# A decoder layer's down projection by Strassen's seven products, with GpSimd making the operand sums

## The chip, the cores and the metric

One core of one Trainium2 chip runs the whole layer. The metric is device time in microseconds (us) from launch to end, the median of several runs. A core has TensorE (PE, with its weight loads PEld), VectorE (DVE), ScalarE (ACT), GpSimd (POOL) and SyncE (SP, which here only issues DMAs). Each engine works through its own queue in order and waits for others by semaphores. TensorE writes to PSUM, which has eight banks of 128 x 512 f32. The profile shows one execution.

## The reference

One layer: attention and a short convolution feed a first residual, then comes the feed-forward part, which is what the change touches. S = 2048 tokens, D = 1024, DFF = 2816, all f32.

```
x  = x + g1 * (mixed @ w_out)
h2 = rmsnorm(x, norm2_g) * (1 + sc2) + sh2
u  = causal_dwconv(h2 @ w_up, ffn_conv_w)      # w_up: 1024 x 5632, three taps over tokens
u_gate, u_val = split(u, 2)
y  = (silu(u_gate) * u_val) @ w_down           # w_down: 2816 x 1024
x  = x + g2 * y                                # g2: one gate per column
```

## The kernel before

The kernel works by token halves `hv` of 1024 tokens. For each there is an up stage and a down stage, and the four stand in a row at the end: up 0, down 0, up 1, down 1. Before them lie the projections, attention and the output projection, which do not change; a norm of token blocks 0 and 1 (`norm2`) runs beside the latter.

**Up stage** (`up`). DFF is cut into NPAIR = 22 tiles of 128 channels. A tile `i` computes the gate and the value channels for 1024 tokens, itself by Strassen's seven products in f16 high and low parts: seven products of 12 matmuls of 512 columns, 84 in all, into three PSUM accumulators X, Y and Z, of `ps_d` and `ps_u` in turn. Beside tile i, `up_weights(i + 1)` forms the next tile's weights: two 128x1024 loads of w_up on SP's queue, scaled by ScalarE, four sums on VectorE, and high and low parts (ScalarE casts, VectorE subtracts: `high`, `low`). VectorE and ScalarE also read the accumulators, run the convolution (`tap`, `taps`), the silu, and the product of gate and value, in `finish`, which is stepped while the next tile's products run. VectorE has 18 instructions in a tile. Four have an accumulator in PSUM as one operand; the other 14 have both tensors in SBUF. The result, 128 channels x 1024 tokens, is stored to `y_sc[i]` in DRAM. GpSimd has nothing to do in the four stages.

**Down stage** (`down`). Per half there are four parts `n` (two blocks of 512 tokens times two halves of 512 columns), each over 22 tiles: 88 steps. A step loads 128 x 512 of y and 128 x 512 of w_down into one 128x1024 tile (`load_pair`), splits it into a high and a low part in fp32r (`split_pair`: ScalarE, then VectorE), three steps ahead, and runs 12 matmuls: four token tiles of 128, three products each (high by high, high by low, low by high). Four accumulators of `ps_d` gather 22 tiles. `add_gated` then multiplies by the gate and adds x, two VectorE instructions per accumulator, and stores the output. `side` is stepped at every other step: in the first down stage it holds the end of the up stage, `norm2` of token blocks 2 and 3 (in `columns` each of 16 groups is four transposes into the one bank of `ps_n`, which ScalarE then reads), and the first weights of up stage 1.

`K` keeps an instruction at its place in program order; what has none may be moved by the scheduler, as the w_up loads are, which SP issues about a tile ahead.

## Time and profile before

| what | us |
|---|---|
| median of 3 runs (lowest, highest) | 2444.38 (2442.55, 2447.06) |
| span of the profiled execution | 2437.6 |
| first up stage, from about 1144 | 399 |
| first down stage, from about 1543 | 252 |
| second up stage, from about 1795 | 398 |
| second down stage, from about 2193 to the end | 245 |

The profiled execution's span lies 6.8 us below the median of the runs: the time of a run has the start and the end of the program in it, outside the first and last instruction. The clock that TensorE was granted was 0.997 of full speed over the span. An engine's busy time in a stretch says how much of it the engine worked; a group row gives the instructions of one line with their number, sum and mean, and behind the bar the idle time ahead of them with what ended it. Durations of matmuls overlap, so the pace of TensorE is read from the chain, which counts each stretch once.

### The profile page before, as it was taken

What the parts mean: (1) busy time and instruction counts of PE and PEld (TensorE: products, weight loads), DVE (VectorE), ACT (ScalarE), POOL (GpSimd) and SP (SyncE); (2) the same over time, 40 slices, a digit from 0 to 9 for tenths busy, and PEclk for the clock granted to TensorE, in tenths of its full rate; (3) what the DMA queues carried; (4) which work ended last, traced back from release to release, by engine and by line L of the source; (5) the groups of instructions that cost most, each with busy time, mean ns of one, the idle gap of its engine ahead of it and who ended that gap; (6) DMA issues with size and microseconds to landing.
All of it is one profiled execution on the core that took longest, in us unless ns stands there. A gap on an engine that the chain in (4) does not pass through costs nothing.

```text
span 2437.6 us, 38399 instructions
## 1 busy us (share of the span) xinstructions
PE 2360.2 (97%) x14451; PEld 1586.8 (65%) x14451; DVE 1772.6 (73%) x3329; ACT 1261.4 (52%) x2024; POOL 336.6 (14%) x282
## 2 busy tenths in 40 slices
PE   5999999999899998999999999999999999999999
PEld 5988788888677776444444444788864444448887
DVE  6566884542799987456888888757768888885554
ACT  4433443221588887343665665554546556554333
POOL 0111011011577884001000000000000000000000
PEclk9999999999999999999999999999999999999999
DMA  9344686543599997434222222676742222236775
GB/s 278 118 122 126 181 235 189 155 139 95 116 185 184 225 181 153 166 113 147 84 89 87 87 87 87 204 245 216 229 134 87 87 87 88 93 103 209 229 227 183
DMA packets 428706, 368.70 MB, mean 151 GB/s; under 512 B 184208, under 2 KB 327912, under 8 KB 427496
## 3 DMA queue, kind: packets, MB, share of 16 engines
q1 hardware_dynamic: 421400, 349.40, 51.4%
q10 hardware_dynamic: 4752, 8.46, 1.0%
q0 software_dynamic: 2368, 8.39, 0.9%
q8 instruction: 113, 1.85, 0.3%
q14 instruction: 73, 0.60, 0.1%
HBM read 267.54 MB, written 65.08 MB: 136 GB/s over the span
## 4 chain that ended last, share of the span: by engine, by line
PE 82%; DVE 7%; issue 5%; ACT 3%; DMA 2%; POOL 1%; SPq 0%; ACTq 0%; DVEq 0%; POOLq 0%
PE acc L1256 33%; PE acc L142 27%; PE pr L142 11%; PE pv L142 3%; PE pt L937 2%; PE ps L876 1%; PE ps L877 1%; DVE near L944 1%; PE po L973 1%; DVE s_t L900 1%; ACT s_t L917 1%; PE po L975 1%; PE po L974 1%; PE pt L1097 1%; ACT near L939 0%
## 5 line engine op out<-in xcount | busy, mean ns | idle before, releaser
L1256 PEld LDWEIGHTS <-pair 128*128 128x128 f16 x3696 | 361.6, 98 | 436.1 <-issue 0.3
L1256 PE MATMUL acc<-t,pair 128*128 128x512 f16 x2112 | 477.4, 379 | 0.0
L1256 PE MATMUL acc<-b,pair 128*128 128x512 f16 x1584 | 363.4, 379 | 0.0
L1228 DVE TENSOR_TENSOR lo<-raw,hi 128x1024 fp32r<-128x1024 f32 x176 | 211.8, 1222 | 153.6 <-ACT hi L1227 151.5
L142 PE MATMUL acc<-hi 128*128 128x512 f32 x704 | 276.7, 393 | 1.6 <-DVE t L1073 1.6
L142 PE MATMUL acc<-lo,hi 128*128 128x512 f32 x704 | 274.2, 390 | 0.5 <-DVE lo L1228 0.5
L1227 ACT ACTIVATE hi<-raw 128x1024 fp32r<-128x1024 f32 x176 | 182.4, 1055 | 178.1 <-PE acc L142 142.3
L142 PE MATMUL acc<-hi,lo 128*128 128x512 f32 x704 | 274.2, 389 | 0.0
L1269 DVE SCALAR_TENSOR_TENSOR w<-w,fcw,w 128x1024 f32<-128x1024 f32 x176 | 226.1, 1284 | 34.7 <-ACT w L1264 25.4
L1080 ACT ACTIVATE pair<-raw 128x1024 f16<-128x1024 f32 x132 | 138.3, 1049 | 68.3 <-DVE raw L1163 68.3
L142 PE MATMUL acc<-wp,mp 128*128 128x512 f16 x768 | 171.1, 382 | 1.1 <-DVE raw L829 1.0
L1264 ACT ACTIVATE w<-w,fcw 128x1024 f32<-128x1024 f32 x88 | 100.7, 1144 | 130.7 <-DVE w L1162 130.7
L917 ACT ACTIVATE s_t<-s_t,nb,cst 128x2048 f32<-128x2048 f32 (+15 forms) x128 | 164.7, 1288 | 4.8
L1083 DVE TENSOR_TENSOR pair<-raw,pair 128x1024 f16<-128x1024 f32 x132 | 160.7, 1217 | 4.7 <-ACT pair L1080 4.7
L608 ACT ACTIVATE wx<-wx 128x512 f32<-128x512 f32 x88 | 55.6, 632 | 203.7 <-DMA wx<-in_w_up_dram 173.9
L142 PE MATMUL pr<-hh,wh 128*128 128x512 f32 x384 | 153.3, 399 | 0.0
L142 PEld LDWEIGHTS acc<-hi 128*128 128x128 f32 x704 | 132.2, 188 | 31.5 <-DVE t L1073 4.4
L142 PE MATMUL pr<-hh,wl 128*128 128x512 f32 x384 | 150.8, 393 | 0.6 <-DVE wl L179 0.6
L142 PE MATMUL pr<-hl,wh 128*128 128x512 f32 x384 | 151.0, 393 | 0.0
L142 PEld LDWEIGHTS acc<-hi,lo 128*128 128x128 f32 x704 | 132.2, 188 | 27.7
L142 PEld LDWEIGHTS acc<-lo,hi 128*128 128x128 f32 x704 | 132.2, 188 | 27.6 <-DVE lo L1228 1.1
L929 POOL TENSOR_TENSOR wide<-s_t,wide 128x1024 f16<-128x1024 f32 x64 | 136.7, 2136 | 5.3
(296 smaller groups left out, 4680.9 us busy)
## 6 DMA issues: line engine op xcount, KB each, us to landing
raw<-in_w_up_dram SPq DMA_DIRECT2D x88, 512.0 KB, 3.9
raw<-y_sc SPq DMA_DIRECT2D x176, 256.0 KB, 4.2
raw<-in_w_down_dram SPq DMA_DIRECT2D x176, 256.0 KB, 5.5
wx<-in_w_up_dram SPq DMA_DIRECT2D x88, 256.0 KB, 2.9
y_sc<-w SPq DMA_DIRECT2D x44, 512.0 KB, 2.6
wm<-in_w_ada_dram SPq DMA_DIRECT2D x128, 128.0 KB, 2.9
wr<-in_w_in_dram SPq DMA_DIRECT2D x40, 256.0 KB, 4.2
x_t<-in_x_dram SPq DMA_DIRECT2D x16, 512.0 KB, 5.7
```

What stands on the lines that cost most here:

```text
L142: ins = T.matmul(acc, lhsT=a, rhs=b, start=st, stop=sp)
L608: K(A.activation(t, t, AF.Abs, accum_out=l1[:, n : n + 1]))
L917: K(A.activation(cols, cols, AF.Exp, bias=nb[:, p : p + 1], scale=qk[:, 4:5], accum_out=un["l"][:, p : p + 1]))
L929: K(G.tensor_tensor(wide[:, 1, :], s_t[:, WB * P : WU], wide[:, 0, :], op=ALU.subtract))
L937: K(T.transpose(pt[:, b * P : (b + 1) * P], s_t[:, (b0 + b) * P : (b0 + b + 1) * P], ident))
L1080: K(A.activation(hi, raw, AF.Copy))
L1083: K(V.tensor_tensor(lo, raw, hi, op=ALU.subtract))
L1227: K(A.activation(hi, raw, AF.Copy))
L1228: K(V.tensor_tensor(lo, raw, hi.bitcast(F32), op=ALU.subtract))
L1256: K(T.matmul(acc, lhsT=a, rhs=b, start=st, stop=sp, skip_group_check=True))
L1264: K(A.activation(y, u[:, 0:1024], AF.Copy, scale=fcw[:, ct : ct + 1]))
L1269: K(V.scalar_tensor_tensor(y, u[:, m : m + 1024], fcw[:, m * 44 + ct : m * 44 + ct + 1], y, op0=ALU.mult, op1=ALU.add))
```

## The change

The down stage computes the same product by seven products in place of eight. For a pair j of channel tiles (2j and 2j + 1, NJ = 11 pairs), of y with a and b for its two blocks of 512 tokens and of the gated w_down with its two column halves, it needs seven y operands and seven w operands: b11, b21, b22 and the sums t1 to t4 on the one side, a11, a12, a22 and the sums s1 to s4 on the other.

- In the up stage `finish` writes the product of gate and value into a tile of its own. `down_inputs` stores three parts of it as they are and has GpSimd make t1 at an even tile and t2, t3 and t4 behind an odd one (128x512 f32, four per pair).
- In the first up stage alone, `down_weights` loads two rows of w_down for each pair, has GpSimd multiply them by the gate (two 128x1024 products) and form four 128x512 sums, and keeps them in DRAM for both halves. It is issued at the start of an odd tile.
- The stores of GpSimd's results are issued by SP at the start of the next tile (`store_later`, `flush`).
- `down` has 7 products of 11 steps: 77 steps with one split and 12 matmuls each, as before. Two sets of accumulators alternate, `ps_d` and `ps_u` with the bank of `ps_n`; a set is added to over two or three products, and after each product its four accumulators are read once (`evict`), by ScalarE after the first and by VectorE after the others; GpSimd adds SBUF tiles in twelve places. The output needs no gate any more.
- `side` is stepped at every step, and twice at some; steps that need a bank for transposes run only in the products 1, 3, 4 and 7 (`window`), and the first weights of up stage 1 fill the steps between (`other`).

```diff
-    y_sc = [dram.tile([P, S], F32, name=f"y_sc{i}") for i in range(NPAIR)]
+    y_op = {n: [dram.tile([P, D], F32, name=f"y_{n}_{j}") for j in range(NJ)] for n in ("b11", "b21", "b22", "t1", "t2", "t3", "t4")}
+    w_op = {n: [dram.tile([P, D], F32, name=f"w_{n}_{j}") for j in range(NJ)] for n in ("a11s3", "a12a22", "s1s2", "s4")}
...
-            g = temp()
-            K(V.tensor_tensor(g, acc, gate, op=ALU.mult))
-            K(V.tensor_tensor(src, src, g, op=ALU.add))
-            nc.sync.dma_start(dst, src)
...
+        plan = (("a11", "b11"), ("s2", "t2"), ("a12", "b21"), ("s3", "t3"), ("s1", "t1"), ("a22", "t4"), ("s4", "b22"))
...
+        def load_pair(hv, p, j):
+
+            w, y = plan[p]
+            n, e = place[w]
             raw = raw_tile()
-            K(nc.sync.dma_start(raw[:, 0:512], y_sc[i][:, Q * 512 : (Q + 1) * 512]))
-            K(nc.sync.dma_start(raw[:, 512:1024], w_down[i * P : (i + 1) * P, hf * 512 : (hf + 1) * 512]))
+            K(nc.sync.dma_start(raw[:, 0:512], y_op[y][j][:, hv * 512 : (hv + 1) * 512]))
+            K(nc.sync.dma_start(raw[:, 512:1024], w_op[n][j][:, e * 512 : (e + 1) * 512]))
...
+        def down_inputs(i, hv, y):
+
+            j = i // 2
+            cols = slice(hv * 512, (hv + 1) * 512)
+            a, b = y[:, 0:512], y[:, 512:1024]
+            if i % 2 == 0:
+                t12 = fq.tile([P, 1024], F32, tag="lo", name="t12", bufs=4)
+                K(nc.sync.dma_start(y_op["b11"][j][:, cols], a))
+                gsub(t12[:, 0:512], b, a)
+                store_later(y_op["t1"][j][:, cols], t12[:, 0:512])
...
+            gsub(t12[:, 512:1024], b, t12[:, 0:512])
+            gsub(t34[:, 0:512], b, b12)
+            gsub(t34[:, 512:1024], a, t12[:, 512:1024])
...
+        def down_weights(j):
...
+            for w in (wa, wb):
+                K(G.tensor_tensor(w, w, gates[:, D : 2 * D], op=ALU.mult))
+            gadd(s1, a21, a22)
+            gsub(a21, a11, a21)
+            gsub(s2, s1, a11)
+            gsub(s4, a12, s2)
+            for n, w in (("a11s3", wa), ("a12a22", wb), ("s1s2", wc)):
+                store_later(w_op[n][j], w)
+            store_later(w_op["s4"][j][:, 0:512], s4)
...
-                K(V.tensor_tensor(yv, yg, yv, op=ALU.mult))
-                nc.sync.dma_start(y_sc[i][:, hv * 1024 : (hv + 1) * 1024], yv)
+                y = fq.tile([P, 1024], F32, tag="hi", name="y", bufs=4)
+                K(V.tensor_tensor(y, yg, yv, op=ALU.mult))
+                down_inputs(i, hv, y)
...
+                flush()
+                if hv == 0 and i % 2:
+                    next(wsum)
...
-            todo = [(n, i) for n in range(4 * hv, 4 * hv + 4) for i in range(NPAIR)]
+            todo = [(hv, p, j) for p in range(7) for j in range(NJ)]
...
+                if p == 0:
+                    K(A.activation(u2[t], a, AF.Copy))
+                elif p == 1:
+                    add(u2[t], u2[t], a)
+                elif p == 2:
+                    add(xs[0, 0][t], xs[0, 0][t], a)
+                    write(0, 0, t, xs[0, 0][t])
+                elif p == 3:
+                    add(u3[t], u2[t], a)
+                    gadd(u3[t], u3[t], xs[1, 1][t])
...
+                if j == 0:
+                    if p in (0, 4):
+                        sets["a"] = [ps_d.tile([P, 512], F32, tag="d", name="acc") for _ in range(4)]
+                    elif p in (1, 3):
+                        sets["b"] = [ps_u.tile([P, 512], F32, tag="u", name="acc") for _ in range(3)] + [bank["n"]()]
+                    acc = sets["b" if p in (1, 3, 5) else "a"]
...
-                if e < 3 or e % 2 == 0:
-                    next(side, None)
...
+                window = p in (0, 2, 3, 6) and (p == 0 or j >= 2)
+                spare["bank"] = bank["d" if p == 3 else "n"]
+                for _ in range(2 if p == 2 and j >= 4 else 1):
+                    if need != "bank" or window:
+                        need = next(side, "end")
+                        if need == "end":
+                            next(other, None)
+                    else:
+                        next(other, None)
```

GpSimd's queue at the fourth pair of up 0 (`wd` is w_down, `y` the product of gate and value). Before, its last rows ahead of the program's end are stores of the first residual, and none belongs to the four stages:

```order
L831 DMA x1_sc14_93<-x_q_14753 128x512
L831 DMA x1_sc15_94<-x_q_14754 128x512
L1405 UNCONDITIONAL_BRANCH
L1405 ISA
```

With the change, the same queue has for each pair:

```order
L1298 TENSOR_TENSOR wd_15913<-wd_15913,gates_239 128x1024
L1298 TENSOR_TENSOR wd_15914<-wd_15914,gates_239 128x1024
L1258 TENSOR_TENSOR wd_16026<-wd_15913,wd_15914 128x512
L1261 TENSOR_TENSOR wd_15913<-wd_15913 128x512
L1261 TENSOR_TENSOR wd_16026<-wd_16026,wd_15913 128x512
L1261 TENSOR_TENSOR wd_16027<-wd_15914,wd_16026 128x512
L1261 TENSOR_TENSOR t12_16099<-y_16097 128x512
L1261 TENSOR_TENSOR t12_16099<-y_16252,t12_16099 128x512
L1261 TENSOR_TENSOR t34_16254<-y_16252,y_16097 128x512
L1261 TENSOR_TENSOR t34_16254<-y_16252,t12_16099 128x512
```

Ten instructions per pair are new there; the seventh runs late in the odd tile, the last three in the even tile behind it. In up 1 only these four remain.

TensorE's queue in down 0, at a place where `columns` puts its transposes (`pt`) between the matmuls of two steps. Before, one group of four stands between two steps:

```order
L142 MATMUL acc_17989<-hi_18297,lo_18298 128x512
L1097 MATMUL pt_18364<-ident_117,w4_18090 128x128
L1097 MATMUL pt_18364<-ident_117,w4_18091 128x128
L1097 MATMUL pt_18364<-ident_117,w4_18092 128x128
L1097 MATMUL pt_18364<-ident_117,w4_18093 128x128
L142 MATMUL acc_17986<-hi_18326 128x512
```

With the change, at a place in the third product:

```order
L1479 MATMUL acc_18406<-hi_18980,lo_18981 128x512
L1093 MATMUL pt_19065<-ident_216,w4_18494 128x128
L1093 MATMUL pt_19065<-ident_216,w4_18495 128x128
L1093 MATMUL pt_19065<-ident_216,w4_18496 128x128
L1093 MATMUL pt_19065<-ident_216,w4_18497 128x128
L1093 MATMUL pt_19075<-ident_216,w4_18494 128x128
L1093 MATMUL pt_19075<-ident_216,w4_18495 128x128
L1093 MATMUL pt_19075<-ident_216,w4_18496 128x128
L1093 MATMUL pt_19075<-ident_216,w4_18497 128x128
L1479 MATMUL acc_18403<-hi_19017 128x512
```

Two groups follow each other without a matmul between them; this is so at four places (one in the first product, three in the third).

SP's queue in up 0, at the start of an even tile. Before, the two w_up loads of a tile follow one store:

```order
L1176 DMA raw_16000<-in_w_up_dram 128x8x128
L1282 DMA y_sc6_101<-w4_15873 128x1024
L1176 DMA raw_16142<-in_w_up_dram 128x8x128
L1176 DMA raw_16143<-in_w_up_dram 128x8x128
L1282 DMA y_sc7_102<-w4_16016 128x1024
```

With the change, five stores that wait for GpSimd and two loads stand ahead of them:

```order
L1272 DMA y_b11_5_100<-y_16727 128x512
L1251 DMA w_a11s3_5_177<-wd_16543 128x1024
L1251 DMA w_a12a22_5_188<-wd_16544 128x1024
L1251 DMA w_s1s2_5_199<-wd_16656 128x1024
L1251 DMA w_s4_5_210<-wd_16657 128x512
L1251 DMA y_t1_5_133<-t12_16729 128x512
L1292 DMA wd_16858<-in_w_down_dram 128x1024
L1292 DMA wd_16859<-in_w_down_dram 128x1024
L1172 DMA raw_16999<-in_w_up_dram 128x8x128
```

At the start of an odd tile it is three stores.

123 lines of the change are left out of this document (92 added, 31 removed).

## Prediction

> **What bounds the kernel now.** I read the page's busy row first, then the windows of the four stages that the change touches, then the chain of work in order of time. The columns of the windows are the stretch, its length, and each engine's busy time with its number of instructions.
>
> ```profile
> PE 2360.2 (97%) x14451; PEld 1586.8 (65%) x14451; DVE 1772.6 (73%) x3329; ACT 1261.4 (52%) x2024; POOL 336.6 (14%) x282
> ...
> core 0: us, PE busy (x) PEld busy (x) DVE busy (x) ACT busy (x) POOL busy (x), PEclk, DMA share, GB/s
> 1144.00:1543.00 399.00, 399.00 (x1851) 180.97 (x1849) 347.29 (x388) 233.28 (x346) 1.08 (x2) 1.00 0.28 90
> 1543.00:1795.00 252.00, 249.90 (x1124) 203.99 (x1124) 174.14 (x215) 131.04 (x156) 0.00 (x0) 1.00 0.71 229
> 1795.00:2193.00 398.00, 398.00 (x1846) 180.44 (x1845) 347.31 (x389) 227.68 (x302) 0.00 (x0) 1.00 0.27 88
> 2193.00:2438.00 245.00, 239.90 (x1059) 198.23 (x1057) 130.65 (x123) 91.53 (x87) 0.00 (x0) 1.00 0.67 212
> ...
> 1144.35 398.86 PE acc L1256 x1848
> 1794.64 398.88 PE acc L1256 x1848
> 2193.52 235.32 PE acc L142 x1038
> ```
>
> The stages are, in turn, first up, first down, second up, second down. TensorE has work without a break in all four; in the up stages the chain is one piece of matmuls. A matmul of an up stage takes 398.86 / 1848 = 0.2158 us of the chain, one of a down stage 235.32 / 1038 = 0.2267. But VectorE is close behind in the up stages: 347.3 of 399 us. Per pair of up tiles (11 pairs) it is busy 347.3 / 11 = 31.6 us while TensorE needs 398.86 / 11 = 36.3: a slack of 4.7. GpSimd does nothing there. Its work of the change is put into that slack.
>
> **What the down stages lose.** Each goes from 88 steps of 12 matmuls to 77, so 132 matmuls fewer: 132 x 0.2267 = 29.9 us, twice. The form and the pace stay (same types, same weight loads), and each step still has one split, so VectorE and ScalarE have less to do in step with TensorE. In the second stage nothing but splits lies beside the matmuls:
>
> ```profile
> L1228 DVE TENSOR_TENSOR lo<-raw,hi 128x1024 fp32r<-128x1024 f32 x85 | 103.5, 1224 | 105.5 <-ACT hi L1227 103.7 <-DMA raw<-y_sc 1.5
> ...
> 2432.51 0.39 PE L142 MATMUL acc<-hi,lo 128*128 128x512 f32 x1
> 2432.94 0.69 DVE L1073 TENSOR_TENSOR t<-acc,gates 128x512 f32<-128x512 f32 x1
> 2433.66 0.69 DVE L1074 TENSOR_TENSOR xs<-xs,t 128x512 f32<-128x512 f32 x1
> ```
>
> VectorE idles 105 us between its splits, so the twelve GpSimd additions of that stage find room. At the end one of two VectorE instructions behind the last matmul goes: 0.7. Second down: **-30.6**.
>
> The first down stage also carries the norm of token blocks 2 and 3, with 64 transposes. Before, a step of it came at every other matmul step; now it comes at every step, in product 3 partly two at once, and those with transposes in products 1, 3 and 4 alone.
>
> ```profile
> L1099 ACT ACTIVATE t<-pt,sh,a 128x512 f32<-128x512 f32 x16 | 12.4, 776 | 39.3 <-PE pt L1097 39.3
> ...
> L1083 DVE TENSOR_TENSOR t<-t,t 128x512 f16<-128x512 f32 x16 | 10.6, 686 | 0.0
> ```
>
> At four places eight transposes now stand in a row on one bank, so the second four wait for the first's 0.78 us eviction: 4 x 0.78 = 3, and 4 with ScalarE's queue in front. For block 3 VectorE has 11 half-tile instructions of 0.69 per column group and four splits of 1.22: 12.5 us, beside four steps of 12 x 0.2267 = 10.9 and their transposes: about 1 short, four times. So 8 of the 29.9 come back (bounds 0 and 22, for work that lies behind other work altogether and for a double step that waits through a split too): first down **-22**.
>
> **What the first up stage gains.** Per pair of tiles GpSimd gets two 128x1024 products with the gate and eight 128x512 sums. The nearest rows, and what GpSimd does to VectorE's instructions:
>
> ```profile
> L929 POOL TENSOR_TENSOR wide<-s_t,wide 128x1024 f16<-128x1024 f32 x64 | 136.7, 2136 | 5.3
> L745 POOL TENSOR_TENSOR wo<-wo,gates 128x512 f32<-128x512 f32 x16 | 20.5, 1282 | 1.3 <-DMA wo<-in_w_out_dram 1.3
> ...
> L928 POOL TENSOR_SCALAR wide<-s_t 128x1024 f16<-128x1024 f32 x64 | 66.9, 1045 | 79.2 <-ACT s_t L917 77.2 <-DMA far<-wide 1.1
> ...
> L136 POOL TENSOR_SCALAR th<-tf x32: 617/618/752, 172.7 to 369.7; 128x512 f16<-128x512 f32 x32
> ...
> L782 DVE SCALAR_TENSOR_TENSOR wp<-wo,rim,wp x16: 739/743/1319, 951.0 to 990.0; 128x512 f16<-128x512 f32 x16
> ...
> 956.66 2.13 POOL L929 TENSOR_TENSOR wide<-s_t,wide 128x1024 f16<-128x1024 f32 x1
> ...
> 957.01 0.69 DVE L944 TENSOR_TENSOR near<-pt,near 128x512 f16<-128x512 f32 x1 [0.37 <-ACT near L939]
> ...
> 958.02 1.32 DVE L782 SCALAR_TENSOR_TENSOR wp<-wo,rim,wp 128x512 f16<-128x512 f32 x1
> ...
> L128 DVE TENSOR_TENSOR rqt<-rqt,r x96: 155/166/608, 162.4 to 361.7; 128x8 f32<-128x8 f32 x96
> ...
> 251.59 0.68 DVE L179 TENSOR_TENSOR wl<-wr,wh 128x512 fp32r<-128x512 f32 x1
> ...
> 252.04 0.75 POOL L136 TENSOR_SCALAR th<-tf 128x512 f16<-128x512 f32 x1 [2.52 <-ACT tf L501]
> ...
> 252.19 0.61 DVE L128 TENSOR_TENSOR rqt<-rqt,r 128x8 f32<-128x8 f32 x1
> ```
>
> (The three numbers of a source row are the shortest, median and longest in ns.) A sum is L745's form: 1.28. For the product I double that and take off one start: from 512 to 1024 elements a GpSimd scalar instruction grows from 0.618 to 1.045, so 0.19 is start: 2 x 1.28 - 0.19 = 2.37 (bounds 2.14, by L929 which writes f16, and 2.56). Per pair 2 x 2.37 + 8 x 1.28 = 15.0 us.
>
> That work is not free for VectorE. At 958.02 an instruction with two tensors in SBUF starts while GpSimd's L929 runs until 958.79, and ends at 959.34: 1.32 us in place of 0.743. It did its work behind GpSimd's end, and only 0.19 of it was hidden. The other way round: GpSimd's instruction at 252.04 took 0.75 in place of 0.618, as it waited for the VectorE instruction that ran until 252.27, and then VectorE's at 252.19, which takes 0.166 alone, waited for GpSimd's end at 252.79. So the two exclude each other, whole instructions, and the first to ask goes first. L944, with one operand in PSUM, runs its usual 0.69 inside the same L929: such instructions don't mind.
>
> In an up tile VectorE has 18 instructions; by the group rows below, 4 of them read an accumulator, at 0.68, and 14 have both tensors in SBUF.
>
> ```profile
> L1269 DVE SCALAR_TENSOR_TENSOR w<-w,fcw,w 128x1024 f32<-128x1024 f32 x85 | 109.2, 1284 | 17.2 <-ACT w L1264 12.7
> ...
> L1162 DVE TENSOR_TENSOR t<-t,acc 128x512 f32<-128x512 f32 x44 | 29.9, 680 | 4.6 <-PE acc L1256 4.6
> L1162 DVE TENSOR_TENSOR w<-t,acc 128x512 f32<-128x512 f32 x43 | 29.4, 684 | 23.0 <-PE acc L1256 23.0
> ```
>
> A GpSimd instruction starts behind some VectorE instruction and holds up the next one. It costs VectorE its length, less 0.10 of its own that is hidden (0.75 - 0.23 of wait = 0.52 of 0.618), less 0.19 hidden of VectorE's, less 0.13 for the 4 cases in 18 in which the next reads PSUM and runs beside it (4/18 x 0.6): a sum 0.86, a product 1.95. Per pair 8 x 0.86 + 2 x 1.95 = 10.8. Of VectorE's idle time most goes once it is late (23.0 us were waits for TensorE); I leave 0.4 per pair for waits on ScalarE. VectorE then needs 31.6 + 10.8 + 0.4 = 42.8 against TensorE's 36.3: 6.5 per pair, 71 for eleven, less 2.6 for the last three sums, which run in the down stage: **+69**. It reaches TensorE because every tile's accumulators are read and its weights split by VectorE in order. ScalarE and GpSimd have room in 42.8 us. The bounds are 0 (all of it under PSUM reads and idle time) and 116 (the 4.7 of idle time stays as it is).
>
> The Trainium skill's page "SBUF — State Buffer", section "SBUF: two separate sides", has a rule that speaks against this change: a VectorE instruction with two SBUF inputs and a GpSimd one that reads SBUF lock a shared pair of ports for the whole instruction, and the loser is fully blocked. By that rule taken whole, with nothing hidden at the starts, the time would be that of rival 5; the trace agrees with the lock, and shows 0.10 and 0.19 hidden.
>
> In the second up stage only the four sums of y remain: 4 x 0.86 = 3.4 per pair, under the slack of 4.7: **0** (up to +10 where three fall on one tile). On SP's queue the stores that wait for GpSimd now stand ahead of the w_up loads:
>
> ```profile
> 1306.82 4.85 SPq L1176 DMA_DIRECT2D raw<-in_w_up_dram  x2
> ...
> 1325.98 2.17 ACT L1182 ACTIVATE raw<-raw,cst 128x1024 f32<-128x1024 f32 x2
> ...
> raw<-in_w_up_dram SPq DMA_DIRECT2D x88, 512.0 KB, 3.9
> ```
>
> They land by 1306.82 + 4.85 + 3.9 = 1315.6 and are used at 1325.98: 10 us cover the few issues in front, and a GpSimd that is late by up to that. Cost 0. DMA: the stage adds some 40 MB in 399 us to 90 GB/s, 190 in all; the down stage carries 229 today.
>
> **Sum**, against the profiled execution: 2437.6 - 22 - 30.6 + 69 = 2454.0. The median of the runs stands 6.8 above this span, so 2460.8.
>
> **Rivals.**
> (1) VectorE keeps the port: GpSimd gets it only when VectorE turns to one of the PSUM reads, and so overlaps 0.6 each time. A sum then costs 0.39, a product 1.48, a pair 6.1; VectorE needs 38.1, 1.8 over TensorE, +20: 2412. This is the case on the other side. The sign turns where a GpSimd instruction costs VectorE 0.93 on average (mine: 10.8 / 10 = 1.08). For it: back-to-back VectorE instructions overlap their starts; against: at 252 GpSimd had asked first and went first.
> (2) Sums hide altogether, no exclusion: 2392. L944's 0.69 is for it, L782's 1.32 against.
> (3) VectorE's idle time stays, as its waits on ScalarE (12.7 us at L1269) grow with the tile: +116, 2508.
> (4) The first down stage is bound by its norm work and keeps its length, +22: 2483.
> (5) Nothing is hidden at the starts: 8 x 1.15 + 2 x 2.24 = 13.7 per pair, VectorE at 45.7, +100: 2492. Against it stand 0.52 of 0.618 and 1.32 of 0.77 + 0.743.
> That TensorE would not do fewer matmuls is excluded by the program.
>
> **How the numbers follow.** Forecast 0.50; its own range is 2439 to 2484 (0.95 to 1.15 per GpSimd instruction: -14 and +8; the first down stage giving back 0 to 23 in place of 8). Rival 1 0.22; 2 0.04; 3 0.11; 4 0.06; 5 0.07. The range reaches from just below rival 1 to just short of rival 3: 2410 to 2502. About 0.2% (4.9 us) is what a measurement tells from no change. Rivals 1 and 2 are faster, but for a little: 0.25. Rivals 3, 4 and 5 are slower, 0.24, and of the forecast's 0.50 all that lies above 2449, 0.40: 0.64. The forecast's low end is the same: 0.11.
>
> **What would show it.** In the first up stage: over 440 us for 1848 matmuls, TensorE waiting on VectorE, VectorE's 1.22 and 1.28 us groups with means above 1.5 while those that read accumulators stay at 0.68; the second up stage at 399. First down near 229, second near 215 with 924 matmuls each. I am wrong if the first up stage stays under 420 (rivals 1, 2) or VectorE's instructions keep their lengths, or if the first down stage stays above 240.

## The result and the profile after

The changed kernel takes 2510.51 us (2504.18 to 2515.56), against 2444.53 (2442.55 to 2447.06) in the runs beside it: ratio 1.0275, 95% interval 1.0253 to 1.0297, slower. The forecast was 2461, with 2502 as the upper end. The side held, and so did the mechanism of the first up stage; two other terms of the sum did not. The profiled execution took 2508.74, its span is 2507.0. So a run's time has 1.7 us outside its span, and the like holds for every execution whose time is given with its span. The 6.8 that the forecast added to its span was for the most part the distance between the median and a quicker execution.

The stage lengths below run from one stage's first matmul to the next one's, read from the records:

| stage | before | after | change | forecast |
|---|---|---|---|---|
| start of up 0 | 1144.2 | 1147.0 | +2.8 | 0 |
| up 0 | 398.7 | 476.0 | +77.3 | +69 |
| down 0 | 251.6 | 256.5 | +4.9 | -22 |
| up 1 | 398.7 | 412.6 | +13.9 | 0 |
| down 1 with its tail | 244.4 | 215.0 | -29.4 | -30.6 |

So of the 53 us by which the span (2507.0 against 2454.0) misses, 27 lie in down 0, 14 in up 1, 8 in up 0, 3 ahead of it and 1 in down 1. The 3 ahead of up 0 are no effect of the change: in the changed kernel, a1 to a4, e1 and n1, which share all that lies there, up 0 starts between 1143.1 and 1149.1.

First the page's busy row after the change, then the windows of the same four stages (stretch, length, then each engine's busy time and number of instructions, the granted clock, DMA).

```profile
PE 2340.5 (93%) x14187; PEld 1549.9 (62%) x14187; DVE 1890.4 (75%) x3291; ACT 1240.9 (49%) x2010; POOL 696.4 (28%) x460
```

```profile
core 0: us, PE busy (x) PEld busy (x) DVE busy (x) ACT busy (x) POOL busy (x), PEclk, DMA share, GB/s
1147.00:1623.00 476.00, 420.17 (x1850) 184.45 (x1848) 453.63 (x389) 230.87 (x345) 231.94 (x109) 0.96 0.46 157
1623.00:1879.00 256.00, 232.55 (x989) 185.79 (x988) 161.44 (x195) 123.50 (x149) 24.69 (x15) 0.95 0.62 208
1879.00:2292.00 413.00, 400.70 (x1852) 180.82 (x1850) 386.17 (x388) 226.62 (x301) 78.54 (x41) 1.00 0.31 103
2292.00:2507.00 215.00, 210.37 (x926) 173.30 (x924) 115.82 (x104) 81.56 (x80) 24.99 (x15) 1.00 0.66 221
```

In up 0 VectorE is busy for 453.6 of 476 us and TensorE has breaks; in down 0 neither is full, and the granted clock is 0.95. Down 1 alone is as it was forecast. What TensorE waits for, from the view of waits (line, releaser, sum, times, longest), up 0 first, then down 0:

```profile
PE acc L1319 <- DVE t L1158: 55.8, 30, 4.2
...
PE acc L1479 <- DVE lo L1231: 8.4, 9, 3.0
PE pt L1093 <- DVE w L1117: 8.0, 7, 5.2
PE pt L1093 <- ACT t L1095: 5.6, 4, 3.0
PE acc L1479 <- ACT hi L1230: 1.1, 4, 0.4
```

In up 0 there is one wait: TensorE wants an accumulator back that VectorE (line 1158) has not read yet. 398.7 + 55.8 is 454.5; most of the rest to 476 is the clock, 0.04 x 476 = 19. VectorE's and GpSimd's groups over nine pairs of up tiles of up 0 say why VectorE is late (behind the bar the busy time and the mean in ns):

```profile
L1332 DVE SCALAR_TENSOR_TENSOR w<-w,fcw,w 128x1024 f32<-128x1024 f32 x73 | 119.9, 1642 | 6.0 <-ACT w L1327 3.4
L1078 DVE TENSOR_TENSOR pair<-raw,pair 128x1024 f16<-128x1024 f32 x54 | 84.1, 1558 | 0.0
L1159 DVE TENSOR_TENSOR raw<-t,raw 128x512 f32<-128x512 f32 x18 | 29.5, 1637 | 0.6
L1158 DVE TENSOR_TENSOR w<-t,t 128x512 f32<-128x512 f32 x18 | 24.8, 1376 | 1.9
L1158 DVE TENSOR_TENSOR w<-t,acc 128x512 f32<-128x512 f32 x36 | 24.4, 678 | 0.4 <-PE acc L1319 0.4
...
L1261 POOL TENSOR_TENSOR wd<-wd 128x512 f32<-128x512 f32 x27 | 58.3, 2171 | 1.4
L1298 POOL TENSOR_TENSOR wd<-wd,gates 128x1024 f32<-128x1024 f32 x18 | 50.1, 2804 | 0.0
```

Instructions with both operands in SBUF grew, from 1284, 1217, 692 and 693 ns in the same groups of the kernel before to 1642, 1558, 1637 and 1376; the read of an accumulator stayed at 678 (684 before). Two groups with both operands in SBUF kept their length, the product of gate and value (1217) and one sum (685); in b2 below, at the place shown there, both fall beside GpSimd's work and take 2.28 and 1.16 us. Summed over all groups VectorE's instructions are 10.2 us longer per pair of tiles; the forecast had 10.8. GpSimd's own instructions grew too, from 1.28 in the forecast's row to 2.1 for a sum of the weights and 1.9 for one of y; in down 0 the last three sums, of which the first starts at 1633.83, take 1.3 each.

One place in up 0, from the timelines of VectorE and of TensorE (start, length, instruction) and the windows around it:

```profile
1213.70 3.61 DVE L1332 SCALAR_TENSOR_TENSOR w<-w,fcw,w 128x1024 f32<-128x1024 f32 x2
1217.22 0.68 DVE L1158 TENSOR_TENSOR t<-t,acc 128x512 f32<-128x512 f32 x1
...
1217.96 4.35 PE L1319 MATMUL acc<-t,pair 128*128 128x512 f16 x12 [3.13 <-DVE t L1158]
```

```profile
1214.80:1217.80 3.00, 0.03 (x1) 0.00 (x0) 2.96 (x3) 1.20 (x2) 0.10 (x1) 1.00 0.62 175
1217.80:1221.20 3.40, 3.24 (x8) 1.13 (x8) 3.37 (x5) 1.11 (x2) 0.76 (x1) 0.50 0.00 0
```

Two convolution instructions take 3.61 us in place of 2 x 1.284; the read of the accumulator stands behind them in VectorE's queue; TensorE waits 3.13 us for it; and then it runs 3.4 us at half clock, so that twelve matmuls take 4.35 us, where such a row takes 2.75 at full clock.

In down 0 the seven products took 42.2, 30.1, 49.2, 38.5, 36.6, 29.9 and 29.9 us. The worst two, the first and the third, begin the same way. The timelines of SP, ScalarE, VectorE and TensorE in product 1 and then in product 3:

```profile
1635.60 2.08 SPq L1106 DMA_DIRECT2D w<-x_sc  x4
1641.21 1.06 ACT L1110 ACTIVATE junk<-w 128x1024 bf16<-128x1024 f32 x1 [2.81 <-DMA w<-x_sc]
1643.55 1.04 ACT L1230 ACTIVATE hi<-raw 128x1024 fp32r<-128x1024 f32 x1
...
1714.86 1.29 SPq L1106 DMA_DIRECT2D w<-x_sc  x3
1719.45 1.06 ACT L1110 ACTIVATE junk<-w 128x1024 bf16<-128x1024 f32 x1 [0.82 <-DMA w<-x_sc]
1723.13 1.99 ACT L1230 ACTIVATE hi<-raw 128x1024 fp32r<-128x1024 f32 x2
1724.20 1.23 DVE L1231 TENSOR_TENSOR lo<-raw,hi 128x1024 fp32r<-128x1024 f32 x1 [5.35 <-ACT hi L1230]
1728.62 1.05 PE L1093 MATMUL pt<-ident,w 128*128 128x128 f32 x2 [5.25 <-DVE w L1117]
```

The norm's loads of x1 (line 1106) are issued, and the squares (line 1110) stand in ScalarE's queue one step of 2.72 us later: they wait for the loads. The next split (line 1230) stands behind them, VectorE's half of it (1231) behind that, and the chain of root and scale (1113 to 1117) behind that one; the transposes that want the scaled columns then hold TensorE for 5.25 us. The two places differ in one thing. In product 1 the first square waits 2.81 us for its load. In product 3 only 1.0 us of waiting is for loads (0.82 and 0.19); there the double step puts all four squares, 5.6 us from 1717.50 to 1723.13, in one row in front of the split.

The waits of down 0 add up to 23.1 us, and a granted clock of 0.95 over 256 us is up to 13 more. Before, the same stage had 2.1 us of waits and the full clock.

### The profile page after: what moved, and what is told of

Its sections match the earlier page's. It is cut to its first block, busy times and chain, and to the rows that moved or that the text cites. A ratio compares the mean times of both kernels' runs of the same rounds, so it can differ in the third digit from the quotient of the medians.

```text
span 2507.0 us, 38366 instructions
## 1 busy us (share of the span) xinstructions
PE 2340.5 (93%) x14187; PEld 1549.9 (62%) x14187; DVE 1890.4 (75%) x3291; ACT 1240.9 (49%) x2010; POOL 696.4 (28%) x460
## 5 line engine op out<-in xcount | busy, mean ns | idle before, releaser
L1319 PE MATMUL acc<-t,pair 128*128 128x512 f16 x2112 | 494.8, 388 | 68.1 <-DVE t L1158 68.1
L1332 DVE SCALAR_TENSOR_TENSOR w<-w,fcw,w 128x1024 f32<-128x1024 f32 x176 | 255.1, 1450 | 21.9 <-ACT w L1327 14.1
L1230 ACT ACTIVATE hi<-raw 128x1024 fp32r<-128x1024 f32 x154 | 160.3, 1055 | 193.1 <-PE acc L1479 79.2
L1479 PE MATMUL acc<-lo,hi 128*128 128x512 f32 x550 | 217.9, 396 | 9.2 <-DVE lo L1231 9.2
L1479 PE MATMUL acc<-hi 128*128 128x512 f32 x550 | 219.5, 399 | 1.3 <-ACT hi L1230 1.1
L1479 PE MATMUL acc<-hi,lo 128*128 128x512 f32 x550 | 216.6, 394 | 0.0
L1078 DVE TENSOR_TENSOR pair<-raw,pair 128x1024 f16<-128x1024 f32 x132 | 182.2, 1381 | 2.6 <-ACT pair L1075 2.6
L1261 POOL TENSOR_TENSOR t<-y,t 128x512 f32<-128x512 f32 x44 | 81.8, 1859 | 355.2 <-DVE y L1345 355.2
L1261 POOL TENSOR_TENSOR t<-y 128x512 f32<-128x512 f32 x44 | 83.7, 1902 | 280.5 <-DVE y L1345 280.5
L902 DVE CUSTOM_DVE_ANT_0 s_t<-ps,nf,mx 128x512 f32<-128x512 f32 (+1 forms) x192 | 119.5, 643 | 16.7 <-PE ps L881 8.4
```

Of the source, the lines that this page charges most:

```text
L902: K(V.tensor_tensor_reduce(out=s_t[:, o0 + c0 : o0 + c0 + cw], in0=ps[:, 0:cw], in1=nf[:, c0 : c0 + cw], scale=1.0, scalar=-3.0e38 if g == ...
L1078: K(V.tensor_tensor(lo, raw, hi, op=ALU.subtract))
L1230: K(A.activation(hi, raw, AF.Copy))
L1261: K(G.tensor_tensor(o, a, b, op=ALU.subtract))
L1319: K(T.matmul(acc, lhsT=a, rhs=b, start=st, stop=sp, skip_group_check=True))
L1332: K(V.scalar_tensor_tensor(y, u[:, m : m + 1024], fcw[:, m * 44 + ct : m * 44 + ct + 1], y, op0=ALU.mult, op1=ALU.add))
```

## The experiments

All are told by the ratio to the kernel before on the same chip, since its median moved between 2438.7 and 2444.5. Stages are in us, from one profiled execution of each kernel. How well a stage repeats shows in down 0 of the changed kernel, a3 and e1, which leave that stage's program alone: 256.3 to 256.5. By their ratios alone a5, d1 and d2 can't be told apart; they are compared by stages.

| kernel | ratio (95% interval) | up 0 | down 0 | up 1 | down 1 |
|---|---|---|---|---|---|
| before | 1 | 398.7 | 251.6 | 398.7 | 239.7 |
| changed | 1.0275 (1.0253 to 1.0297) | 476.0 | 256.5 | 412.6 | 211.2 |
| a1 narrow weight operations | 1.0019 (1.0009 to 1.0029) | 412.6 | 255.3 | 412.6 | 211.3 |
| a2 all narrow | 0.9894 (0.9878 to 0.9909) | 398.7 | 253.2 | 398.7 | 210.0 |
| a3 own tiles | 1.0251 (1.0235 to 1.0267) | 468.7 | 256.3 | 412.6 | 210.7 |
| a4 one step | 1.0242 (1.0225 to 1.0259) | 473.9 | 251.3 | 412.6 | 211.3 |
| a5 spaced | 1.0205 (1.0185 to 1.0225) | 475.5 | 241.5 | 412.6 | 211.3 |
| e1 one operand | 1.0054 (1.0039 to 1.0069) | 421.8 | 256.4 | 412.6 | 211.2 |
| b2 y on VectorE | 1.0239 (1.0222 to 1.0256) | 489.2 | 242.7 | 403.4 | 210.1 |
| b3 all on VectorE | 0.9965 (0.9951 to 0.9979) | 418.7 | 242.2 | 403.4 | 211.4 |
| n1 norm out (products + norm) | 1.0435 (1.0419 to 1.0450) | 476.5 | 212.7 + 75.0 | 421.2 | 211.3 |
| b4 spread sums | 0.9944 (0.9931 to 0.9957) | 417.8 | 247.0 | 398.7 | 213.0 |
| d1 lows off VectorE | 1.0191 (1.0156 to 1.0225) | 475.9 | 238.8 | 412.6 | 211.2 |
| d2 narrow additions | 1.0188 (1.0152 to 1.0224) | 476.2 | 235.9 | 412.6 | 211.3 |
| l1 split ahead | 1.0245 (1.0230 to 1.0260) | 476.1 | 249.2 | 412.6 | 213.1 |
| b5 b4, split ahead | 1.0056 (1.0042 to 1.0070) | 417.8 | 259.3 | 398.7 | 221.7 |

**a1 and a2: is it GpSimd's length, or what came with it?** The operations stay, but over 8 columns. All loads and stores stay at their sizes; what is stored is in part taken from the loaded tiles, so the down stages' operands are not the reference's.

```diff
-                K(G.tensor_tensor(w, w, gates[:, D : 2 * D], op=ALU.mult))
-            gadd(s1, a21, a22)
+                K(G.tensor_tensor(w[:, c8], w[:, c8], gates[:, D : D + 8], op=ALU.mult))
+            gadd(s1[:, c8], a21[:, c8], a22[:, c8])
...
-            gsub(t34[:, 0:512], b, b12)
+            gsub(t34[:, 0:8], b[:, 0:8], b12[:, 0:8])
```

> The six GpSimd operations on w_down of each pair of tiles (two gate products over 1024 columns, four sums over 512) are cut to 8 columns; all loads and stores of the same sizes stay, so the products of the down stages are not the reference's. Theory (GpSimd operations on two SBUF operands hold VectorE's like operations back for nearly their length, and that is what fills the first up stage): the first up stage falls from 476 us to what the second has, 410 to 418; the second stays at 411 to 414; the first down stage loses part of what it pays at its start (the sums no longer hold the lo and hi slots for long) and is 240 to 256; the run is 2433 to 2455. Rival A (the added loads and stores on SP and the DMA queues fill the stage): it stays within 5 us of 476 and the run within 10 of 2510. Rival B (half clock after TensorE stalls that have another cause): it stays above 450.

> As the kernel with narrow weight operations, and the four sums of y of each pair, in both up stages, cut to 8 columns too, with every store still made (from y itself): no GpSimd work of length is left in the up stages, and the outputs are not the reference's. Theory: both up stages come back to the 398.7 us of before, 397 to 403; against the kernel with narrow weight operations alone the second up stage loses 10 to 15 and the first about as much; the run is 2405 to 2430. Rival A (stores and loads): the second up stage stays at 410 to 414, the first near 476. Rival B (a fixed cost per GpSimd instruction, whatever its width): the stages fall by less than half of that.

With the weight operations narrow up 0 is 412.6, to the tenth what up 1 has; with all narrow both are back at 398.7. The window of up 0 in the second kernel has TensorE without a break, VectorE as before the change, and the DMA traffic twice that of before (183 GB/s against 90):

```profile
1144.00:1542.00 398.00, 398.00 (x1846) 180.50 (x1845) 347.72 (x388) 233.02 (x345) 52.30 (x108) 1.00 0.53 183
```

So all 77.3 and all 13.9 us come with GpSimd's length; loads and stores cost nothing in either stage. And down 0 hardly moved (255.3 and 253.2): its loss is of another kind. a2 is also what the change would give without the price of its sums, 0.9894: a bound and no version, since it leaves the sums out.

**e1: which GpSimd operations hold VectorE?** The six weight operations of each pair become operations on one operand, at the same widths.

```diff
-            gadd(s1, a21, a22)
-            gsub(a21, a11, a21)
+            gone(s1, a22)
+            gone(a21, a11)
...
+        def gone(o, a):
+            K(G.tensor_scalar(o, a, 1.0, 0.0, op0=ALU.mult, op1=ALU.add))
```

> The six GpSimd operations on w_down of each pair are replaced by operations on one SBUF operand of the same widths (times 1, plus 0), with the same loads and stores, so the down stages' operands are not the reference's. Theory A (what holds VectorE back is two operands on GpSimd): the first up stage falls to about what the second has, 410 to 420, though GpSimd works 1.0 to 1.7 us on each; the run is 2435 to 2455. Theory B (any GpSimd operation over 512 or 1024 columns in SBUF excludes VectorE's two-operand operations): it falls only as far as the operations are shorter (1.65 us for 1024 columns in the kernel before against 2.77, and 0.8 to 1.7 for 512 against 2.1), to 435 to 470. Theory C (GpSimd work of this kind costs the same whatever it is): 470 to 480.

GpSimd still works for long on each; from its groups in up 0, and VectorE's convolution step beside them:

```profile
L1258 POOL TENSOR_SCALAR wd<-wd 128x512 f32<-128x512 f32 x40 | 62.1, 1570 | 1.7
...
L1258 POOL TENSOR_SCALAR wd<-wd 128x1024 f32<-128x1024 f32 x19 | 27.8, 1479 | 0.0
...
L1335 DVE SCALAR_TENSOR_TENSOR w<-w,fcw,w 128x1024 f32<-128x1024 f32 x76 | 105.2, 1384 | 6.1 <-ACT w L1330 2.7
```

Yet up 0 is 421.8: 9.2 us above a1, the kernel without their length, where the two-operand forms cost 63.4. Of the 9.2 the last tile alone has 5.6 (23.5 against 17.9); of the 63.4 it has 11.6. Theory A holds but for these 9, which put the stage just above its 410 to 420. The Trainium skill, "SBUF — State Buffer", section "SBUF: two separate sides", has a VectorE instruction with two SBUF inputs and any GpSimd instruction that reads SBUF exclude each other. Here the two-operand forms did so, and the one-operand ones hardly. One row of the prediction speaks the other way: at 252.19 a short VectorE instruction ended with a one-operand GpSimd instruction, one that writes f16, where those of e1 write f32. No run separates the two.

**a3: the shared tiles.** t1 to t4, s1, s2 and s4 move from the ring of the split operands to idle tiles; t3 is also made ahead of t2.

```diff
-                t12 = fq.tile([P, 1024], F32, tag="lo", name="t12", bufs=4)
+                t12 = [fb.tile([P, 512], F32, tag=f"src{t}", name="t12") for t in range(2)]
```

> The same computation and order of the GpSimd work but for t3, now ahead of t2; the sums t1 to t4, s1, s2 and s4 lie in seven tiles of the source pool that are idle in the up stages, and no longer in the ring of four that the split operands of the down stages use. Theory (27 us of the first down stage's missing gain, and of the last up tile, are partly waits for slots of that ring, held until stores that stand behind a waiting store on SP): the last tile of the first up stage falls from 30.1 us to 23 to 25, the first product of the first down stage from 42.2 to 31 to 36, the run to 2493 to 2503. Rival (the start of the down stage waits for the data itself: y, its sums and their stores, which come as late as before): last tile and first product together fall by less than 4 us and the run stays at 2507 to 2514.

The last tile of up 0 fell from 29.5 to 22.9 us, about as expected; the first product of down 0 stayed, 41.8 against 42.2. Half of this theory fell.

**a4 and a5: how the norm is stepped.** a4 takes the double steps away, a5 also puts two empty steps between the loads of x1 and their squares.

```diff
-                for _ in range(2 if p == 2 and j >= 4 else 1):
+                for _ in range(1):
...
-                yield
+                for _ in range(3):
+                    yield
```

> The work beside the third product of the first down stage (second normalisation of the other half) is advanced once a step in place of twice from step 4 on; nothing else differs, and what is left of it comes after the last product's steps. Theory (third product 49.2 us and the two after it 38.5 and 36.6, because two steps of the normalisation in one product's step put its chain of square, reciprocal root and scale in front of the transposes, and the pause then halves the clock): the third product falls to 33 to 40, the fourth and fifth to 31 to 36, and some of it comes back at the start of the second up stage (up to 8): the run is 2493 to 2506. Rival (the normalisation's own length bounds the stage, wherever it is stepped): the products get shorter but the second up stage starts later by as much, and the run stays at 2505 to 2515 or grows.

> Nothing of the computation changes: the normalisation beside the first down stage is advanced once a step throughout, and two empty steps (5.4 us) stand between its loads of x1 and its squares on ScalarE. Theory (in the changed kernel the squares are queued on ScalarE one step behind loads that take 4.6 us or more to land, and the split of the next operand pair is queued behind the squares, so TensorE starves, then runs at half clock): the first product falls from 42.2 us to 30 to 34, the third from 49.2 to 31 to 36, the fourth and fifth to 30 to 35, and the first down stage from 256.5 to 222 to 236; the second up stage starts at most 5 us late; the ratio to before falls from 1.0275 to 1.014 to 1.020. Rival (the length of the normalisation itself, more work on ScalarE and VectorE than the shorter stage has room for, bounds the stage): some products get shorter, others longer, and the stage stays at 248 to 257.

The double step was worth 5.2 us of down 0: product 3 fell from 49.2 to 32.9, products 4 and 7 grew to 42.4 and 37.4, where 31 to 36 was expected for the fourth. The distance was worth another 9.8: product 1 fell from 41.1 to 35.4, products 4 and 7 to 40.0 and 35.0. Product 3 gained nothing by it (33.4). Together they give back 15 of the 45 us by which down 0 exceeds down 1, where a5 was expected to bring 20 to 34: the distance explains the first product, the double step the third, and neither is enough for the fourth, fifth and seventh.

**n1: the norm by itself.** Down 0 runs without it, and it follows alone.

```diff
-            down(hv, *((last, iter(())) if hv else (chain(last, steps[2], steps[3]), first_weights())))
+            down(hv, *((last, iter(())) if hv else (last, first_weights())))
+            if hv == 0:
+                for _ in chain(steps[2], steps[3]):
+                    pass
```

> The changed kernel, with the second normalisation of the other half taken out of the first down stage and run by itself between it and the second up stage; the computation is the same. Theory (everything that the first down stage loses against the 211 us of the second, 45 us, comes from that normalisation running beside it): its seven products take 30 to 33 us each and together 211 to 216; the normalisation alone then stands in front of the second up stage, and the time from the end of the products to the first matmul of that stage is what it is worth, 45 to 90 us; the run is 2490 to 2560. Rival (the start of the stage, its loads and the shared tiles have a part of their own): the first product stays at 37 or more, or the fourth and fifth at 35 or more, without the normalisation beside them.

The windows of down 0 in this kernel: the first product, the next five, and the last with the norm behind it.

```profile
1621.00:1654.00 33.00, 31.50 (x134) 24.56 (x134) 22.16 (x22) 18.08 (x21) 3.78 (x3) 1.00 0.66 212
1654.00:1804.00 150.00, 150.00 (x664) 124.29 (x663) 82.58 (x75) 59.24 (x57) 21.32 (x12) 1.00 0.71 239
1804.00:1908.50 104.50, 48.79 (x195) 35.84 (x194) 50.26 (x89) 42.74 (x63) 0.00 (x0) 0.65 0.33 106
```

Without the norm the products take 33.1, five times 29.9 and, by the same pace, 30: 212.7. The theory held: with GpSimd's twelve additions, the evictions and the stores still there, all but the 3 us of the first product is hidden. So 256.5 - 212.7 = 43.8 us of the changed kernel's down 0 is the norm, which alone takes some 75 us and 8.6 more in the next stage's first tile (26.7 against 18.1).

**d1 and d2: what of the norm's room.** Both start from a5. d1 takes 20 low halves off VectorE (a one-operand GpSimd copy in their place, without the subtraction), d2 narrows all of GpSimd's additions to 8 columns.

```diff
-                low(b2, *b22)
+                low2(b2, *b22)
...
-                    gadd(u3[t], u3[t], xs[1, 1][t])
+                    gadd(u3[t][:, 0:8], u3[t][:, 0:8], xs[1, 1][t][:, 0:8])
```

> As the kernel with the spaced normalisation (first down stage 241.5 us), but the low halves of the columns that the fourth quarter's normalisation makes (20 operations of 0.69 us on VectorE) are made on GpSimd by a one-operand copy: the subtraction is left out there, so the low halves are not the reference's. Theory (what is left of the first down stage's excess, 30 us, is VectorE's queue: in the steps of the sums it has 12 operations of 0.69 beside four splits of 1.22, 13 us, in the 10.9 that four steps take): the fourth, fifth and seventh products fall from 40.0, 37.8 and 35.0 us to 31 to 36 each and the stage to 226 to 235. Rival (the chain from engine to engine, transpose, ScalarE, VectorE and back, bounds it, whoever does the halves): the stage stays within 3 us of 241.5 or grows.

> As the kernel with the spaced normalisation, with GpSimd's twelve additions over 512 columns in each down stage cut to 8 columns (the outputs then lack most of u2 and x1 in three blocks). Theory (they hold VectorE's split and sums back at the end of the fourth product, where records of 1.5 to 1.7 us stand beside 0.69): the fifth product, 37.8 us with a pause of 3.7 at its start, falls to 32 to 35, and the stage from 241.5 to 235 to 239; the second down stage stays at 211. Rival (they cost nothing, since VectorE has room in the down stages): the stage stays within 2 us of 241.5.

d2's theory held: products 4 and 5 fell from 40.0 and 37.8 to 37.0 and 35.0, the stage by 5.6. Two of VectorE's sums, first in a5, beside four GpSimd additions, then the same two in d2:

```profile
1762.93 5.92 POOL L1259 TENSOR_TENSOR u<-u,xs 128x512 f32<-128x512 f32 x4 [126.06 <-DMA raw<-y_t]
1764.56 1.47 DVE L1085 TENSOR_TENSOR t<-t,t 128x512 f32<-128x512 f32 x1
1766.07 1.66 DVE L1085 TENSOR_TENSOR t<-t,b 128x512 f32<-128x512 f32 x1
...
1760.93 0.68 DVE L1085 TENSOR_TENSOR t<-t,t 128x512 f32<-128x512 f32 x1
1761.64 0.69 DVE L1085 TENSOR_TENSOR t<-t,b 128x512 f32<-128x512 f32 x1
```

d1's theory fell: 2.7 us in place of 6 to 15, although VectorE was given 14 us of room. VectorE's low halves are not what bounds the rest; GpSimd's copies may have taken a part of the gain back, which no run shows.

**l1: more lead for the split.** On a5, three steps ahead in place of two (`e + 3` covers the present step and two more, here and in the kernel before).

```diff
-                while split < min(e + 3, len(todo)):
+                while split < min(e + 4, len(todo)):
```

> As the kernel with the spaced normalisation (first down stage 241.5 us); operand pairs are split three steps ahead of their matmuls in place of two, in the same rings of four. Theory (what is left of the excess is a chain from engine to engine: the split on ScalarE stands behind a column operation that waits for transposes, which stand on TensorE behind the step before, and with VectorE's sums behind it the chain is longer than the two steps of 2.72 us by which the split runs ahead): one step more covers it, the first, fourth, fifth and seventh products fall to 30 to 34 each, the stage to 220 to 232. Rival (rings of four are full then, so ScalarE waits for TensorE's step before to end, and the column operations stand behind that): the stage stays at 238 or more.

Down 0 got worse, 249.2, with product 1 at 43.4: the rival's case, at least as to the result. With rings of four full, the lead cannot be tried cleanly, so the chain from engine to engine is neither shown nor excluded by it.

**b2, b3, b4, b5: toward a better version.** b2 (on a3 and a5) has VectorE make y's sums; b3 has it make the weights' sums too, from the ungated w_down, with the gate applied where the products leave PSUM; b4 spreads the eight sums four to a tile; b5 is b4 with l1's lead.

```diff
-                gsub(t12[0], b, a)
+                sub(t12[0], b, a)
...
-            for w in (wa, wb):
-                K(G.tensor_tensor(w, w, gates[:, D : 2 * D], op=ALU.mult))
-            gadd(s1, a21, a22)
+            add(s1, a21, a22)
...
+            def add_gated(o, a, n):
+                K(V.tensor_tensor(a, a, gate(n), op=ALU.mult))
+                add(o, o, a)
```

> The spaced normalisation, the sums in their own tiles, and the four sums of y of each pair made by VectorE itself in place of GpSimd; w_down's six operations stay on GpSimd. Theory (a sum over 512 columns costs VectorE 0.69 us itself and about 0.9 to 1.2 when GpSimd makes it beside): the second up stage falls from 412.6 us to 398 to 401, as 31.6 us of VectorE work a pair plus 4 x 0.69 = 34.4 stays under TensorE's 36.3; the first, with 34.4 plus about 7.5 of holding by the weight operations, is 452 to 466; the first down stage 222 to 236; ratio to before 1.001 to 1.009. Rival (moving the sums to VectorE costs it as much as it frees): second up stage 408 to 416, first 470 or more.

> As the kernel with y's sums on VectorE, and the weight sums are made by VectorE too, of the ungated w_down (four sums a pair, no gate products); a11, a12 and a22 are read straight from w_down in the down stages, and the gate multiplies the product sums when they leave PSUM (two VectorE operations there in place of one, and 12 tiles multiplied once more in SBUF). GpSimd has nothing left in the up stages. Theory: VectorE 31.6 + 8 x 0.69 = 37.1 us a pair against TensorE's 36.3, so the first up stage is 400 to 412; the second 398 to 401; the first down stage 222 to 238, the second 210 to 214 with a tail of 4 to 6: the run is 2378 to 2412, ratio 0.973 to 0.987, faster than both. Rival (stores and loads that stay, or VectorE's longer evictions, take it back): the first up stage above 425 or the first down stage above 248, and the run at 2425 or more.

> As the kernel with all sums on VectorE; of the eight sums of a pair, t4 is made one tile later and s2 one tile later, so that each tile has four, in place of three and five. Theory (the 19.4 and 18.6 us tiles come from five sums in one tile: VectorE then has more than the tile's 18.1 us, which the other tile's slack doesn't pay back): the second up stage falls from 403.4 us to 398 to 401, the first from 418.7 to 408 to 418; the down stages stay within 2 us; the run is 6 to 15 us under the kernel with all sums on VectorE, ratio to before 0.990 to 0.994. Rival (VectorE is bound by its work over the pair, not by its distribution): the first up stage stays within 3 us of 418.7; the second falls all the same or stays at 403.

> As the kernel with the sums on VectorE spread over the tiles (ratio 0.9944, first down stage 247 us, first product 40.5), with operand pairs split three steps ahead in place of two. Theory (the chain between the engines): first down stage 224 to 238, first and second up stage as before at 418 and 399, second down stage 211 to 214; the run is 9 to 23 us shorter, ratio 0.985 to 0.991. Rival (full rings make ScalarE wait): the stage stays at 243 or more and the ratio at 0.993 to 0.998.

b2 missed: up 0 went up to 489.2, where 452 to 466 was expected. Its even tiles take 26 to 28 us and its odd ones 18.1. GpSimd's six operations now run in one burst, and TensorE waits twice per pair, for some 1.3 us and for 5.5 (69.2 us in the stage; most of the other 21 is half clock behind the long ones); GpSimd's and TensorE's timelines:

```profile
1320.52 5.65 POOL L1298 TENSOR_TENSOR wd<-wd,gates 128x1024 f32<-128x1024 f32 x2 [32.65 <-DMA wd<-in_w_down_dram]
...
1332.35 1.59 POOL L1262 TENSOR_TENSOR ws<-wd,ws 128x512 f32<-128x512 f32 x1
...
1340.92 4.42 PE L1321 MATMUL acc<-t,pair 128*128 128x512 f16 x11 [5.46 <-DVE t L1159]
```

VectorE's extra time in this burst, summed over its instructions from 1320.5 to 1335, is about what the theory said (7.2 us against 7.5). But it falls into one tile, where VectorE's three sums of y follow it, and the slack of the other tile could not pay for it. Nor did up 1 reach 399: with one sum in a tile and three in the next it took 403.4, and with four sums of y spread two and two, in b4, 398.7.

b3 is a little faster than the kernel before, at 0.9965, and b4 at 0.9944. b3 missed its forecast of 0.973 to 0.987: up 0 took 418.7 in place of 400 to 412 and down 0 242.2 in place of 222 to 238. b4's windows by stage:

```profile
1144.00:1562.00 418.00, 401.89 (x1851) 180.68 (x1848) 398.32 (x473) 234.23 (x345) 1.08 (x2) 1.00 0.45 151
1562.00:1809.00 247.00, 226.70 (x991) 180.74 (x990) 180.51 (x234) 121.77 (x147) 0.00 (x0) 0.99 0.68 226
1809.00:2207.50 398.50, 398.50 (x1847) 180.59 (x1847) 375.50 (x435) 230.96 (x304) 0.00 (x0) 1.00 0.33 108
2207.50:2425.00 217.50, 210.51 (x926) 173.40 (x924) 138.52 (x147) 81.80 (x80) 0.00 (x0) 0.99 0.66 218
```

In up 1, VectorE with four sums a pair is busy 375.5 of 398.5 and TensorE never waits; in up 0, with eight, it is busy 398 of 418 and TensorE waits 16.1 us for it: spreading changed next to nothing there (418.7 to 417.8), so for that stage the rival held. Down 0 grew by 4.8 us in b4, where 2 were allowed; b4 also moves a group of stores in its first product, which went from 36.7 to 40.5, and no run tests that. b5 lost 12.3 and 8.7 us in the two down stages, more than l1 had (7.7 and 1.8).

## Why the prediction was right and wrong

- **Fewer matmuls: right.** Down 1 with its tail gave 29.4 us back (forecast 30.6), and n1 shows 212.7 for down 0 as well where the norm doesn't run beside it.
- **The lock in up 0: right.** Forecast 42.8 us per pair of tiles; the records show 43.1 (19.7 and 23.4), with VectorE's instructions 10.2 us longer per pair against 10.8 forecast and 1.1 us of idle time left against 0.4. a1 and a2 show that the whole loss is GpSimd's length, e1 that the two operands make most of it. At TensorE this appears as 55.8 us of pauses and 19 of half clock behind them. The clock was not foreseen; as VectorE was busy for 379.4 of the 389 us of nine pairs, it can't have cost much there, but no run takes it away. The 8 us of size are mostly the last tile: the forecast took 2.6 off for the last three sums, and the tile took 29.5 us, 6.1 more than the other odd ones. a3 brings it to 22.9, which points at the ring from which the first splits of down 0 are taken. The prediction took "whole instructions" from two rows, one of them (252.04) with a GpSimd instruction of one operand; e1 shows that in f32 such instructions cost VectorE little.
- **No difference in up 1: wrong.** The step that failed is "3.4 per pair, under the slack of 4.7: 0". The slack was averaged over the pair. GpSimd makes one sum in one tile and three in the next; every second tile took 19.5 us in place of 18.1 and the others stayed. The bound that was kept, "+10 where three fall on one tile", was the right mechanism; its size was +13.9. b4 shows it from the other side: the four sums of y spread evenly, on VectorE, leave 398.7.
- **Down 0 gives back 8 of 29.9: wrong, and half of the miss.** 34.8 came back, more than the upper bound of 22. The forecast counted what VectorE's queue and one bank of transposes would cost the norm beside the splits, 8 us, and let the stage keep the 12 us that it cost before; 20 in all. It was 43.8. The step that failed is the one that takes the stepping as a matter of throughput. Stepping at every step halves the distance from a load to its use: in product 1 loads that land in 4.6 us are waited for in ScalarE's queue, in front of the next split, and a5 gives 9.8 us back. The double step puts the whole chain of squares, root and scale in front of the transposes of product 3, and a4 gives 5.2 back. The forecast also put two things at nothing without a reason. One is the half clock behind the pauses, up to 13 us of the stage (0.95 of 256). The other is GpSimd's additions in the first down stage: it argued for the second one alone that they "find room", which d2 bears out (211.3 with and without), but beside the norm they hold VectorE, and d2 gives 5.6 back. What is left then, 235.9 - 212.7 = 23, is near the 20 that were forecast. In d2 12.4 us of it are still waits of TensorE, for splits (5.8 and 2.2) and for the norm's columns (3.1 and 1.3), at the full clock; the other 11 are close to the 10 that the norm cost before beyond its 2.1 us of waits. The cause of those 12.4 is open: d1 excludes VectorE's low halves as more than 3 us of it, and l1 could not try the chain between the engines without filling the rings.
- **SP's queue and DMA at 0: right** (a2: 398.7 with every store and load made; and in the changed kernel itself no wait of ScalarE from 1160 to 1600 is for a load).
- **Rivals.** Rival 3's 2508 is all but the measured 2510.5, and that is chance: it has VectorE's idle time stay at 4.7 per pair and up 0 grow by 116, where 1.1 and 77.3 were measured. Rival 4 (down 0 keeps its length) named the stage with the largest miss, and was closest for it (+4.9), but has the norm's work as the bound; of the 43.8 us, a4, a5 and d2 take 20.6 away with the norm's work unchanged.

## What to carry to other kernels

Work that is put into the slack of an engine has to fit the slack of each tile in which it runs, not the mean over two: here three GpSimd sums in one tile cost 1.4 us though the pair had room for all four, and on VectorE 0.5, where two and two cost nothing. GpSimd operations on two SBUF operands took about two thirds of their own length from VectorE here (10.2 us of 15.0 per pair), so where VectorE is close behind, VectorE should make such sums itself (0.69 us against a hold of 0.9). And side work that is stepped twice as often has its loads half as far ahead: move the load when the step moves, and keep two steps of it from standing in one row in front of what the main work needs.

## What the hardware showed

- In up 0 and down 0 of the changed kernel TensorE made 13 pauses of 3 us or more; 11 of them ran into 3.4 to 10 us at a granted clock of 0.50. Of 15 pauses between 1 and 2 us one did, and so did the one of 2.96. Up 1, where the longest pause was 1.2 us, and down 1 had no such stretch. So a stall can cost TensorE more than its length: 3.13 us of waiting at 1217.96 brought another 1.6.
- GpSimd's and VectorE's instructions hold each other up in both directions: a GpSimd sum grew from 1.28 to 2.1 us, and VectorE's convolution step from 1.28 to 1.64. GpSimd operations with one operand (f32 to f32), of 1.5 us each, lengthened VectorE's step to 1.38 only and cost 3.6 us over all tiles but the last, where those with two cost 51.8.
